# Reordering the loads and stores of a kernel's prologue, one encoder layer on one Trainium2 core

## The chip, the cores and the metric

The kernel runs on one core of one Trainium2 chip. The metric is the device time of one execution in microseconds (us). The time before the change is the median of 3 runs, 2337.61 us (2336.99 to 2337.95).

Names used below: PE is the matrix engine (TensorE), PEld its loading of stationary operands, DVE the vector engine, ACT the scalar engine, POOL GpSimd, SP the engine that here only issues transfers. A transfer (DMA) is issued by an engine's queue and carried by 16 DMA engines that all queues share.

## The reference, cut to what matters

One layer of an encoder over 4096 prompt frames and 32 sample frames, width 1024, all in float32:

```
h    = rmsnorm(x, norm_g)                      # x: 4096 x 1024 (and 32 x 1024)
proj = h @ w_in                                # w_in: 1024 x 5120 -> u | v | z_a | xb | z_b
v_n  = layernorm(v)
a    = u * (W_s v_n + b) * silu(z_a)           # W_s: 128 x 128 per head, masked in 64-blocks
b    = groupwise_linear(mean_window(xb) - xb) * scale * silu(z_b)    # w_pool: 4 groups of 256 x 256
x    = x + concat(a, b) @ w_out
y    = rmsnorm(x, final_g)
```

The windowed mean and the subtraction work along the frames and the group-wise linear map along the channels, so `w_pool` can be multiplied into the xb columns of `w_in` ahead of everything else. The product, a 1024 x 1024 matrix, is called `comb` in the kernel. For the sample frames the state of earlier frames (`state_pool`, 15 rows) goes through the same map.

## The kernel before, in words

**Products.** Each large product is split in 2 x 2 blocks and done with seven block products (numbered q = 0 to 6) in place of eight. Each float32 operand is split into a high part (a rounding copy on ACT, L120 for weights, L458 for tokens) and a low part (a subtraction on DVE, L82), and three of the four part products are made. One such block product of a stage is 12 matmuls of 128 x 512 (L194). The sums of blocks that the seven products need are subtractions and additions on DVE (L116 for weights, L486 to L495 for tokens).

**Stages.** First comes a prologue, then the v stage (tokens times the v columns of `w_in`, by pairs of 128-frame tiles), then the gate and pool stages over four blocks of 1024 frames, then the two output stages. The change touches the prologue alone, which ends about 56 us into the run.

**The prologue** (L519 to L548) does three things, interleaved over eight steps i = 0 to 7:

- *Rows of comb.* Row tile i of the xb columns of `w_in` (128 x 1024, loaded by `load_rows`, L254) is transposed by eight PE transposes (`comb_rows`, L407), copied out of PSUM (L411; DVE for i = 0 and 1, ACT from i = 2), and multiplied with `w_pool` in 16 matmuls (`comb_times`, L269). ACT copies the result into a tile `outs[i]` (L425), of the tag `xt` for i < 4 and `vt` from i = 4, and POOL's queue stores it to `comb` (L427). The loop traces the transposes of row i + 1 ahead of the matmuls of row i.
- *The v weights.* Four column chunks c = 0 to 3 of the v columns, two tiles of the tag `op` each (`load_v_weights`, L280 and L281), are made into the split operands of the seven products, which stay in `wv`. `PACE` says after which step how many of the 28 pieces are traced.
- *The first pair of token tiles.* `pairs[0].load` (L445) loads two tiles of x; `norms` squares and sums them on ACT (L302), makes the reciprocal root with short DVE instructions (L312, L87 to L92), and multiplies the tiles in place by it and by the gain `g_bc` (L315). Then PE transposes quarters of the tiles (L452) and `split` makes the operands, seven more `op` tiles.

Beside these, the state rows (`past`) and the last frames with the sample frames (`edge`) are loaded. The loop that follows (L550) multiplies pair n while it prepares pair n + 1.

**Buffers.** A tag has a fixed number of tiles, and a load into a tile waits until its last use is over: `vt` 4, `xt` 4, `op` 9, `h` 6.

**Order.** The source is not the order on the engines. A planner simulates the program and gives each engine the instruction that comes first in the source among those it takes to be ready, so later work can be drawn ahead of work that it believes is still waiting. `tc.keep_in_program_order` ties an instruction behind the one traced before it on its engine. Once planned, each engine works strictly in its given order. The dictionary `before` lists, for each step i, what is traced between the transposes of row i + 1 and the matmuls of row i: loads, norms, parts of `past`.

Of the kernel before, what the change touches and what calls it, by code (L numbers as in the profile page):

```python
# [8 lines left out]
F32 = mybir.dt.float32  # L9
# [3 lines left out]
AF = mybir.ActivationFunctionType  # L13
ALU = mybir.AluOpType

P = 128
# [20 lines left out]
def stream_step(ctx: ExitStack, tc, x_prompt, x_sample, state_pool, norm_g, w_in, ln_v_g, ln_v_b,  # L37
# [9 lines left out]
    nc = tc.nc  # L47
# [13 lines left out]
    comb = dram.tile([D, D], F32, name="comb")  # L61
# [16 lines left out]
    def small(tag, n, rows=P):  # L78
        return smallp.tile([P, 8], F32, tag=tag, name=tag)[:rows, :n]
# [4 lines left out]
    def rsqrt(a, n, rows=P):  # L84

        y, t = small("rs_y", n, rows), small("rs_t", n, rows)
        nc.vector.tensor_single_scalar(t.bitcast(I32), a.bitcast(I32), 1, ALU.logical_shift_right)  # L87
        nc.vector.tensor_scalar(y.bitcast(I32), t.bitcast(I32), -1.0, float(0x5F3759DF), ALU.mult, ALU.add)
        for _ in range(3):
            nc.vector.tensor_tensor(t, y, y, ALU.mult)  # L90
            nc.vector.scalar_tensor_tensor(t, t, -0.5, a, ALU.mult, ALU.mult)
            nc.vector.scalar_tensor_tensor(y, t, 1.5, y, ALU.add, ALU.mult)  # L92
        return y
# [16 lines left out]
    behind = []  # L110
# [108 lines left out]
    with ExitStack() as ph:  # L219
# [8 lines left out]
        def xtile(dt=F32):  # L228
            return xt_p.tile([P, D], dt, tag="xt", name="xt")

        def vtile():
            return v_p.tile([P, D], F32, tag="vt", name="vt")

        def op(dt=F32R):
            return op_p.tile([P, D], dt, tag="op", name="op")

        def half(dt=F32):
            return h_p.tile([P, HALF], dt, tag="h", name="h")

        def acc_tile():  # L240
            return ps_acc.tile([P, 512], F32, tag="acc", name="acc")
# [10 lines left out]
        def load_rows(i):  # L252
            rows_t[i] = vtile()
            nc.sync.dma_start(rows_t[i], w_in[0, i * P:(i + 1) * P, 3 * D:4 * D])  # L254
# [11 lines left out]
        def times(dst, g, rows):  # L266

            for ct in range(2):
                mm(dst, rows[ct], wraw[g // 2][:, 2 * (g % 2) + ct, :], start=ct == 0, stop=ct == 1)  # L269
# [6 lines left out]
        def load_v_weights(c):  # L276
            v_raws[c] = a, b = [t.rearrange("p (k e) -> p k e", e=P)
                                for t in (op(F32), op(F32))]
            c0 = D + c * P
            nc.sync.dma_start(a, w_in_v[:, :, c0:c0 + P])  # L280
            nc.sync.dma_start(b, w_in_v[:, :, c0 + 512:c0 + 512 + P])  # L281

        def make_v_weights():
            for c in range(4):
                a, b = v_raws.pop(c)
                cs = slice(c * P, (c + 1) * P)
                for step in weight_ops(a[:, :4], a[:, 4:], b[:, :4], b[:, 4:],
                                       lambda: half().rearrange("p (k e) -> p k e", e=P),
                                       lambda q: (wv[q][:, 0, :, cs], wv[q][:, 1, :, cs]), c < 2):
                    step()  # L290
                    yield

        def norms(xs_, vs_, behind=False):

            nx, nv, n = len(xs_), len(vs_), len(xs_) + len(vs_)
            rows = (xs_ + vs_)[0][1]
            a = small("na", n, rows)
            if xs_:
                ss = small("ss", nx, rows)
                for i, (xt, _) in enumerate(xs_):  # L300
                    junk = h_p.tile([P, D], BF16, tag="junk", name="junk", bufs=1)
                    nc.scalar.activation(junk[:rows], xt[:rows], AF.Square, accum_out=ss[:, i:i + 1])  # L302
            if vs_:
                st = smallp.tile([P, 2, 2, 6], F32, tag="bn", name="bn")
                mv = smallp.tile([P, 2, 2], F32, tag="mv", name="mv")
                for i, (v, _) in enumerate(vs_):
                    for z in range(2):
                        nc.vector.bn_stats(st[:rows, i, z, :], v[:rows, z * 512:(z + 1) * 512])
                    nc.vector.bn_aggr(mv[:rows, i, :], st[:rows, i].rearrange("p z c -> p (z c)"))
                nc.vector.tensor_scalar_add(a[:, nx:], mv[:rows, :nv, 1], EPS)  # L310
            if xs_:
                nc.vector.tensor_scalar(a[:, :nx], ss, 1.0 / D, EPS, ALU.mult, ALU.add)  # L312
            r = rsqrt(a, n, rows)
            for i, (xt, _) in enumerate(xs_):
                nc.vector.scalar_tensor_tensor(xt[:rows], xt[:rows], r[:, i:i + 1], g_bc[:rows], ALU.mult, ALU.mult)  # L315
            if vs_:
                nb = small("nb", nv, rows)
                nc.vector.scalar_tensor_tensor(nb, mv[:rows, :nv, 0], -1.0, r[:, nx:], ALU.mult, ALU.mult)
                for i, (v, _) in enumerate(vs_):
                    act = nc.scalar.activation(v[:rows], v[:rows], AF.Identity, scale=r[:, nx + i:nx + i + 1],  # L320
                                               bias=nb[:, i:i + 1])
                    if behind:
                        tc.keep_in_program_order(act)
# [34 lines left out]
        class Past:  # L358


            def load(self):
                self.st = half(), half()
                for z in range(2):
                    nc.gpsimd.memset(self.st[z][:HALO], 0.0)
                    nc.sync.dma_start(self.st[z][1:HALO], state_pool[0, 0, :, z * 512:(z + 1) * 512])
# [26 lines left out]
        pairs = []  # L392
        past = Past()
        PACE = (2, 4, 4, 4, 4, 4, 3, 3)

        def edge_load():
            nc.sync.dma_start(edge[:DEC], xs)
            nc.sync.dma_start(edge[DEC:m_edge], xp[SEQ - HALO:SEQ, :])
            nc.sync.dma_start(g_bc, norm_g[0].partition_broadcast(P))

        def comb_rows(i):
# [12 lines left out]
        outs = {}  # L414

        def comb_times(i, cols, halves=(0, 1)):
            if 0 in halves:
                outs[i] = xtile() if i < 4 else vtile()
            out = outs[i]
            for gp in halves:  # L420
                acc = acc_tile()
                for z in range(2):
                    s = [slice((2 * z + ct) * P, (2 * z + ct + 1) * P) for ct in range(2)]
                    times(acc[:, z * 256:(z + 1) * 256], 2 * gp + z, [cols[gp][:, x] for x in s])
                nc.scalar.copy(out[:, gp * 512:(gp + 1) * 512], acc)  # L425
            if 1 in halves:
                nc.gpsimd.dma_start(comb[i * P:(i + 1) * P, :], out)  # L427

        def columns():
            with nc.allow_non_contiguous_dma(reason="a few columns of constants"):  # L430
                tc.keep_in_program_order(nc.sync.dma_start(lvg, ln_v_g[0].rearrange("(h c) -> c h", c=P)))
                tc.keep_in_program_order(nc.sync.dma_start(lvb, ln_v_b[0].rearrange("(h c) -> c h", c=P)))
                tc.keep_in_program_order(nc.sync.dma_start(psc, pool_scale[0].rearrange("(h c) -> c h", c=P)))


        class Pair:
            def __init__(self, b, j):
                self.b, self.j, self.direct = b, j, b == 0 and j >= 2

            def load(self):  # L440
                self.x = []
                for z in range(2):
                    t0 = self.b * TB + z * HALF + self.j * P
                    xt = xtile()
                    nc.sync.dma_start(xt, xp[t0:t0 + P, :])  # L445
                    self.x.append(xt)

# [66 lines left out]
            def store(self, queue=nc.scalar):  # L514
                for z, v in enumerate(self.v):
# [2 lines left out]

        pairs += [Pair(b, j) for b in (1, 2, 3, 0) for j in range(4)]  # L519
        first_steps = pairs[0].operands()  # L520
        before = {0: [lambda: load_rows(3), lambda: load_v_weights(1)],
                  1: [lambda: load_rows(4)],
                  2: [lambda: load_rows(5), lambda: load_v_weights(2), past.load],
                  3: [lambda: load_rows(6), pairs[0].load],
                  4: [lambda: load_rows(7), edge_load],
                  5: [past.split, lambda: load_v_weights(3)],
                  6: [past.times, lambda: norms([(xt, P) for xt in pairs[0].x], []), pairs[1].load],
                  7: first_steps[:2]}
        weights = make_v_weights()
        load_rows(1)  # L530
        load_rows(2)
        load_v_weights(0)
        parts = comb_rows(0)
        for i in range(KT):
            if i == 0:
# [64 lines left out]
    def raw_tile(dt=F32):  # L600
        return raw_p.tile([P, D], dt, tag="raw", name="raw")
# [206 lines left out]
    with ExitStack() as ph:  # L808
# [231 lines left out]
        pairs = [[OutPair(z, i) for i in range(SEQ // (2 * P))] for z in range(2)]  # L1040
# [59 lines left out]
        for n in range(n_sets):  # L1100
# [9 lines left out]
            for m, (s, q) in enumerate(order):  # L1110
# [5 lines left out]
                if n == n_sets - 14 and m == 2:  # L1116
                    rows = raw_tile()[:DEC]
# [32 lines left out]
    with ExitStack() as ph:  # L1150
# [22 lines left out]
        outs = FewRows(lambda k: abT[k, :, SEQ:], lambda k: w_out_v[k], few_columns, KT - 1)  # L1173
# [92 lines left out]
```

## Time and profile before

| | |
|---|---|
| median of 3 runs | 2337.61 us |
| profiled execution, its own time | 2337.89 us |
| span of the profile | 2336.0 us |
| PE busy | 2317.2 us, 99% of the span |
| DVE, ACT, POOL busy | 1774.6, 889.3, 229.2 us |
| transfers | 457.42 MB, mean 196 GB/s |

The span runs from the first to the last instruction; the profiled execution's own time is 1.9 us longer. PE is busy in nearly all of the span, and a busy PE is not a PE at its peak. The average hides the prologue: in its first twentieth the 16 DMA engines move 316 and 310 GB/s, later mostly less than 200. "L254 SPq" is a transfer issued by SP from line 254; "xt<-acc" is written tile and read tile; "<-DMA vt<-in_w_in_dram" names what ended a wait. In the chain of waits, time is followed back from the last instruction to whatever released it.

### The profile page before, as it was taken

To read this page: it belongs to the slowest core of one execution; us is meant where nothing else is said; L and a number is where in the kernel's file an instruction comes from. 1 tells how busy PE (TensorE), PEld (TensorE's weight loads), DVE (VectorE), ACT (ScalarE), POOL (GpSimd) and SP (SyncE) were. 2 spreads that over 40 slices of the span, in tenths; PEclk is the share of its full clock that TensorE was granted. 3 is DMA by queue.
4 is the path that set the end of the run, shared out by engine and by line. 5 is a ranking of instruction groups with operands and counts; after the bars stand their busy time and mean duration, and the time that the engine had idled before them with its cause. 6 is when DMAs were issued, how large, how long until landed. Compare 5 with 4: busy or idle time off the path is not lost.

```text
span 2336.0 us, 32648 instructions
## 1 busy us (share of the span) xinstructions
PE 2317.2 (99%) x11936; PEld 1964.7 (84%) x11936; DVE 1774.6 (76%) x3285; ACT 889.3 (38%) x1596; POOL 229.2 (10%) x412
## 2 busy tenths in 40 slices
PE   8999999999999999999999999999999999999998
PEld 7888888888888888888877899999988777887887
DVE  6888777867887777868668877768776666588887
ACT  7544444334433333433334333334322222233343
POOL 1010000100112000111001211102110000000000
PEclk9999999999999999999999999999999999999999
DMA  8879977335447433483454474435584656846552
GB/s 316 310 269 280 281 244 251 111 108 189 145 170 271 147 127 130 129 328 120 164 164 149 165 276 146 143 94 173 192 323 163 211 201 198 342 163 202 178 167 91
DMA packets 329544, 457.42 MB, mean 196 GB/s; under 512 B 21964, under 2 KB 249932, under 8 KB 326696
## 3 DMA queue, kind: packets, MB, share of 16 engines
q1 hardware_dynamic: 277832, 366.91, 46.9%
q0 software_dynamic: 22288, 73.48, 8.4%
q10 hardware_dynamic: 29264, 14.94, 2.3%
q8 instruction: 94, 1.54, 0.3%
q14 instruction: 66, 0.54, 0.1%
HBM read 286.07 MB, written 169.21 MB: 195 GB/s over the span
## 4 chain that ended last, share of the span: by engine, by line
PE 94%; DMA 3%; DVE 2%; issue 1%; ACT 0%; SPq 0%; DVEq 0%; ACTq 0%
PE acc L194 64%; PE acc L691 8%; PE acc L692 8%; PE acc L693 8%; PE sp L939 2%; PE tr L452 1%; DMA wops<-wop 1%; DMA vt<-in_w_in_dram 1%; DVE wop L82 1%; DMA raw<-abT 1%; PE more L202 1%; DMA op<-in_w_in_dram 0%; PE acc L269 0%; PE acc L202 0%; DMA raw<-in_w_in_dram 0%
## 5 line engine op out<-in xcount | busy, mean ns | idle before, releaser
L194 PE MATMUL acc<-slot,wop 128*128 128x512 f32 (+1 forms) x6720 | 1260.1, 348 | 2.9 <-ACT t L173 1.0
L194 PEld LDWEIGHTS acc<-slot,wop 128*128 128x128 f32 x6720 | 1080.3, 188 | 163.2 <-DVE t L166 6.2
L82 DVE TENSOR_TENSOR wop<-raw,wop 128x512 fp32r<-128x512 f32 x520 | 355.8, 686 | 99.0 <-ACT wop L120 96.3
L120 ACT CAST wop<-raw 128x512 fp32r<-128x512 f32 x360 | 222.8, 622 | 349.2 <-PE acc L194 259.7
L691 PE MATMUL acc<-slot,wop 128*128 128x512 f32 x892 | 348.7, 391 | 1.8 <-DVE y L703 1.8
L693 PE MATMUL acc<-slot,wop 128*128 128x512 f32 x892 | 347.1, 389 | 0.0
L692 PE MATMUL acc<-slot,wop 128*128 128x512 f32 x892 | 347.0, 389 | 0.0
L194 PE MATMUL acc<-slot,op 128*128 128x512 f32 x1344 | 323.5, 395 | 0.1
L194 PEld LDWEIGHTS acc<-slot,op 128*128 128x128 f32 x1344 | 247.6, 188 | 51.8 <-DVE op L82 0.5
L703 DVE TENSOR_TENSOR y<-acc,y 128x512 f32<-128x512 f32 x235 | 159.1, 687 | 128.0 <-PE acc L693 126.9
L166 DVE TENSOR_TENSOR t<-acc,t 128x512 f32<-128x512 f32 (+1 forms) x320 | 185.7, 582 | 85.8 <-ACT t L175 44.9
L691 PEld LDWEIGHTS acc<-slot,wop 128*128 128x128 f32 x892 | 167.4, 188 | 47.0 <-ACT wop L656 11.9
L656 ACT CAST wop<-raw 128x512 fp32r<-128x512 f32 x160 | 99.6, 622 | 259.7 <-PE acc L693 251.9
L693 PEld LDWEIGHTS acc<-slot,wop 128*128 128x128 f32 x892 | 167.4, 188 | 35.2
L692 PEld LDWEIGHTS acc<-slot,wop 128*128 128x128 f32 x892 | 167.5, 188 | 34.2
L82 DVE TENSOR_TENSOR wop<-sum,wop 128x512 fp32r<-128x512 f32 x208 | 142.5, 686 | 57.6 <-ACT wop L120 57.0
L952 POOL DMA_DIRECT2D abT<-t x128 | 69.2, 541 | 822.3 <-DVE t L964 607.9
L120 ACT CAST wop<-sum 128x512 fp32r<-128x512 f32 x144 | 89.4, 622 | 152.6 <-PE acc L194 98.4
L975 DVE TENSOR_TENSOR t<-t 128x527 f32<-128x527 f32 (+3 forms) x160 | 111.0, 697 | 0.5
L656 ACT CAST wop<-sum 128x512 fp32r<-128x512 f32 x64 | 39.9, 623 | 131.6 <-PE acc L693 102.4
L116 DVE TENSOR_TENSOR sum<-raw 128x512 f32<-128x512 f32 x72 | 49.5, 687 | 36.8 <-DMA raw<-in_w_in_dram 34.9
L175 ACT COPY t<-acc 128x512 f32<-128x512 f32 (+1 forms) x80 | 40.1, 503 | 91.0 <-PE acc L194 90.5
(199 smaller groups left out, 1866.1 us busy)
## 6 DMA issues: line engine op xcount, KB each, us to landing
raw<-in_w_in_dram SPq DMA_DIRECT2D x110, 512.0 KB, 4.3
xops<-op SPq DMA_DIRECT2D x72, 512.0 KB, 5.7
abT<-t POOLq DMA_DIRECT2D x128, 256.0 KB, 3.7
raw<-abT SPq DMA_DIRECT2D x64, 512.0 KB, 4.7
slot<-xops SPq DMA_DIRECT2D x30, 1024.0 KB, 9.6
wops<-wop SPq DMA_DIRECT2D x56, 512.0 KB, 3.3
slot<-wops SPq DMA_DIRECT2D x14, 2048.0 KB, 9.9
xt<-in_x_prompt_dram SPq DMA_DIRECT2D x32, 512.0 KB, 4.4
```

What stands on the lines that cost most here:

```text
L82: return nc.vector.tensor_tensor(out, src, hi.bitcast(F32), ALU.subtract)
L116: less = lambda o, x, y: nc.vector.tensor_tensor(o, x, y, ALU.subtract)
L120: pair = nc.scalar.copy(hi, src), lo_part(lo, src, hi)
L166: add = lambda o, x, y: nc.vector.tensor_tensor(o, x, y, ALU.add)
L194: mm(acc, stationary(s, k), moving(m, k), start=fresh and n == 0, stop=n == len(terms) - 1, skip_group_check=True)
L656: nc.scalar.copy(t[:, 0], src)
L691: mm(acc, x[:, 0, k, :], w[:, k, 0, c], start=fresh and k == 0, stop=False, skip_group_check=True)
L692: mm(acc, x[:, 0, k, :], w[:, k, 1, c], start=False, stop=False, skip_group_check=True)
L693: mm(acc, x[:, 1, k, :], w[:, k, 0, c], start=False, stop=k == 3, skip_group_check=True)
L703: nc.vector.tensor_tensor(y, self.acc[bank], y, ALU.add)
L952: nc.gpsimd.dma_start(abT[row, :, t0:t0 + HALF], t[:, :HALF])
L975: tt(nxt[:, lo:HALO + m], s[:, lo:HALO + m], s[:, lo - step:HALO + m - step], ALU.add)
```

## The change

Seven edits, all in the prologue:

1. The stores of `outs[0]` to `outs[3]` leave POOL's queue at the end of each step. They are issued together by SP from step 5, in a new function `comb_store`. Rows 4 to 7 are stored as before.
2. Chunk 0 of the v weights is loaded ahead of row 2, and chunk 1 ahead of row 3.
3. The first token pair is loaded in step 1 in place of step 3, into two `op` tiles in place of `xt` tiles.
4. The gain `g_bc` gets a load of its own in step 2; it had been the last of the edge loads in step 4. The other edge loads move to step 6, behind the load of the second pair.
5. Chunk 3 is loaded in step 4, ahead of row 7, in place of step 5.
6. The norms of the first pair are traced in step 4 in place of step 6, and their two squares are tied behind the ACT instruction traced before them.
7. `past.load` stays in step 2, behind the loads of row 5 and of the gain.

```
@@ norms @@
-        def norms(xs_, vs_, behind=False):
+        def norms(xs_, vs_, behind=False, pinned=False):
...
-                    nc.scalar.activation(junk[:rows], xt[:rows], AF.Square, accum_out=ss[:, i:i + 1])
+                    square = nc.scalar.activation(junk[:rows], xt[:rows], AF.Square, accum_out=ss[:, i:i + 1])
+                    if pinned:
+                        tc.keep_in_program_order(square)
@@ edge_load @@
             nc.sync.dma_start(edge[DEC:m_edge], xp[SEQ - HALO:SEQ, :])
+
+        def g_load():
             nc.sync.dma_start(g_bc, norm_g[0].partition_broadcast(P))
@@ comb_times @@
-            if 1 in halves:
+            if 1 in halves and i >= 4:
                 nc.gpsimd.dma_start(comb[i * P:(i + 1) * P, :], out)
+
+        def comb_store():
+            for i in range(4):
+                nc.sync.dma_start(comb[i * P:(i + 1) * P, :], outs[i])
@@ Pair.load @@
-            def load(self):
+            def load(self, tile=xtile):
...
-                    xt = xtile()
+                    xt = tile()
@@ the prologue's loop @@
-        before = {0: [lambda: load_rows(3), lambda: load_v_weights(1)],
-                  1: [lambda: load_rows(4)],
-                  2: [lambda: load_rows(5), lambda: load_v_weights(2), past.load],
-                  3: [lambda: load_rows(6), pairs[0].load],
-                  4: [lambda: load_rows(7), edge_load],
-                  5: [past.split, lambda: load_v_weights(3)],
-                  6: [past.times, lambda: norms([(xt, P) for xt in pairs[0].x], []), pairs[1].load],
+        before = {0: [lambda: load_v_weights(1), lambda: load_rows(3)],
+                  1: [lambda: pairs[0].load(lambda: op(F32)), lambda: load_rows(4)],
+                  2: [lambda: load_v_weights(2), lambda: load_rows(5), g_load, past.load],
+                  3: [lambda: load_rows(6)],
+                  4: [lambda: load_v_weights(3), lambda: load_rows(7),
+                      lambda: norms([(xt, P) for xt in pairs[0].x], [], pinned=True)],
+                  5: [past.split, comb_store],
+                  6: [past.times, pairs[1].load, edge_load],
                   7: first_steps[:2]}
         weights = make_v_weights()
         load_rows(1)
+        load_v_weights(0)
         load_rows(2)
-        load_v_weights(0)
```

## The prediction

> **What bounds the kernel now.** I read the page, then the chain of waits over the first 70 us, then PE's order of time there, then tables by stretch of time. The page first:
>
> ```profile
> span 2336.0 us, 32648 instructions
> PE 2317.2 (99%) x11936; PEld 1964.7 (84%) x11936; DVE 1774.6 (76%) x3285; ACT 889.3 (38%) x1596; POOL 229.2 (10%) x412
> PE 94%; DMA 3%; DVE 2%; issue 1%; ACT 0%; SPq 0%; DVEq 0%; ACTq 0%
> ```
>
> PE bounds the run as a whole, so the prologue can give back only time in which PE waits or runs slowly. In the chain (start, duration, what) it is not PE that leads there:
>
> ```profile
> 3.19 5.89 DMA vt<-in_w_in_dram
> ...
> 10.28 1.73 PE acc L269 x8
> ...
> 12.18 9.59 DMA vt<-in_w_in_dram
> ...
> 30.79 7.44 DMA op<-in_w_in_dram
> ```
>
> Row 1 lands at 9.08 (3.19 + 5.89), row 4 at 21.77, and chunk 3 holds the chain to 38.23. PE in order of time (start, duration, then what):
>
> ```profile
> 11.85 1.04 PE L407 MATMUL tr<-ident,vt 128*128 128x128 f32 x8
> ...
> 16.18 1.04 PE L407 MATMUL tr<-ident,vt 128*128 128x128 f32 x8
> 17.05 3.62 PE L269 MATMUL acc<-op,h 128*128 128x256 f32 x16
> 21.90 1.06 PE L407 MATMUL tr<-ident,vt 128*128 128x128 f32 x8 [1.23 <-DMA vt<-in_w_in_dram]
> ...
> 31.56 0.66 PE L370 MATMUL tr<-ident,h 16*128 16x16 f32 x8
> 32.15 3.72 PE L269 MATMUL acc<-op,h 128*128 128x256 f32 x16
> 36.28 1.39 PE L407 MATMUL tr<-ident,vt 128*128 128x128 f32 x8 [0.41 <-ACT h L411]
> 37.59 1.06 PE L383 MATMUL acc<-op,h 128*16 128x256 f32 x16
> 38.58 3.72 PE L269 MATMUL acc<-op,h 128*128 128x256 f32 x16
> 44.15 0.66 PE L452 MATMUL tr<-ident,xt 128*128 128x128 f32 x4 [1.85 <-DVE xt L315]
> 44.64 0.60 PE L269 MATMUL acc<-op,h 128*128 128x256 f32 x2
> 45.44 0.80 PE L452 MATMUL tr<-ident,xt 128*128 128x128 f32 x4 [0.20 <-DVE xt L315]
> 46.03 4.74 PE L269 MATMUL acc<-op,h 128*128 128x256 f32 x14
> ...
> 52.84 10.79 PE L194 MATMUL acc<-slot,op 128*128 128x512 f32 x43
> 63.47 0.60 PE L452 MATMUL tr<-ident,xt 128*128 128x128 f32 x4
> ```
>
> Row 0's matmuls end at 12.01 (10.28 + 1.73), the last row's at 50.77 (46.03 + 4.74): 38.76 us. The work between, without waits, is six turns of a row at 0.87 (17.05 - 16.18), 5.22; seven times 16 matmuls at 3.62, 25.34; the state rows at 0.59 (32.15 - 31.56) and 0.99 (38.58 - 37.59), 1.58; two quarters of x at 0.49 (44.64 - 44.15), 0.98. That is 33.12, so 5.64 us are waiting or slowness: 1.23 for row 4, 0.41, 1.85 and 0.20 for the norm, and 1.57 because the last 14 matmuls took 4.74 where 14/16 of 3.62 is 3.17. The remaining 0.38 is spread. By stretch of time (columns: bounds, length, busy times of PE, PEld, DVE, ACT and POOL, granted clock, DMA share, GB/s):
>
> ```profile
> 4.00:16.00 12.00, 10.54 (x59) 8.73 (x58) 5.29 (x9) 3.18 (x6) 0.67 (x1) 1.00 1.07 366
> 16.00:38.30 22.30, 20.59 (x130) 17.15 (x128) 18.08 (x30) 19.52 (x39) 3.10 (x6) 1.00 1.07 390
> 18.45:21.86 3.41, 2.22 (x11) 1.61 (x9) 3.18 (x6) 3.41 (x8) 1.51 (x3) 1.00 1.06 378
> 42.34:45.76 3.42, 1.41 (x9) 1.04 (x10) 3.35 (x6) 3.35 (x8) 0.00 (x0) 1.00 0.24 96
> 45.76:49.17 3.41, 3.41 (x11) 2.78 (x10) 3.41 (x7) 3.41 (x8) 0.53 (x1) 0.50 0.42 157
> 12.05:50.81 38.76, 35.00 (x194) 28.68 (x192) 31.85 (x59) 33.71 (x68) 4.83 (x9) 0.96 0.91 336
> 56.04:2336.00 2279.96, 2267.86 (x11668) 1924.48 (x11668) 1736.19 (x3214) 850.39 (x1521) 223.18 (x396) 1.00 0.57 193
> ```
>
> The slowness is a half clock, 0.50, in the 3.41 us right after a stretch in which PE worked 1.41 of 3.42. To 38.3 us the DMA engines are full: a 512 KB load costs 0.524 MB / 366 = 1.43 us, from 16 us on 1.34.
>
> **The change part by part.** *The stores leave the load stream.* Four stores are 4 x 1.34 = 5.4 us of DMA time that no longer lies before chunk 3. *New order of loads.* Counted from row 1 at 9.08, the queue now holds chunk 0 (two loads), row 2, chunk 1, row 3, the first pair, row 4, chunk 2, row 5, the gain, row 6, chunk 3, row 7. Row 2 lands at 9.08 + 3 x 1.43 = 13.4, row 3 at 17.7, then with 1.34 row 4 at 21.7, row 5 at 25.7, row 6 at 28.4, chunk 3 at 31.1, row 7 at 32.5.
>
> PE reaches row 2 at 12.01, as its first transposes in the old trace show, and starts them at 13.5 now: a new wait of 1.5, and all that follows in PE's order waits with it. Then it needs row 3 at 13.5 + 0.87 + 3.62 = 18.0, row 4 at 22.5, row 5 at 27.0, row 6 at 31.5, row 7 near 36.6: each has landed 0.3 to 4 us before. So the old wait for row 4 goes, a larger one comes at row 2.
>
> *The first pair earlier, its squares tied.* It lands at 20.4 (17.7 + 2 x 1.34), the gain at 27.1. The squares come behind the copies of row 5, near 29. Rows of ACT and POOL before:
>
> ```profile
> 12.94 0.67 POOL L427 DMA_DIRECT2D comb<-xt  x1 [11.63 <-ACT xt L425]
> 16.07 0.62 ACT L120 CAST slot<-op 128x512 fp32r<-128x512 f32 x1 [1.42 <-DMA op<-in_w_in_dram]
> 32.56 1.06 ACT L302 ACTIVATE junk<-xt 128x1024 bf16<-128x1024 f32 x1 [2.12 <-DMA xt<-in_x_prompt_dram]
> 38.26 0.62 ACT L120 CAST slot<-op 128x512 fp32r<-128x512 f32 x1 [0.54 <-DMA op<-in_w_in_dram]
> 44.31 1.06 ACT L302 ACTIVATE junk<-xt 128x1024 bf16<-128x1024 f32 x1
> ```
>
> The square stood in ACT's order 2.12 us ahead of its data, and the casts behind it stood with it. There the second square came right behind the cast of 38.26 and PE could turn the pair at 44.15, 5.9 later. Now the second square stands near 30, so the pair is ready near 36, and PE asks for it near 42. So 1.85 and 0.20 go, and with them the empty stretch that I take for the cause of the half clock: 1.57 more. If this cover fails, up to 3.62 come back.
>
> [...]
>
> ```profile
> 19.86 1.28 DVE L82 TENSOR_TENSOR slot<-op,slot 128x512 fp32r<-128x512 f32 x2
> 29.11 0.69 DVE L116 TENSOR_TENSOR h<-op 128x512 f32<-128x512 f32 x1
> 113.56 0.70 PE L334 MATMUL tr<-ident,et 48*128 48x48 f32 x8
> ```
>
> *Buffers.* With the pair in `op` tiles, eight of nine are taken when chunk 2 is loaded; its second half waits for chunk 0's, whose last subtraction is the first of the two from 19.86, done about 20.5. It lands some 7 us later (the depth of the queue, from chunk 3: issued 30.79, landed 38.23), near 28; DVE first wants it at 29.11 in the old order. Hidden, 1 us of cover. *SP* issues four more transfers, ahead of them everything that PE needs; behind them stand the second pair and the edge frames. The `xt` tiles of the second pair come free only when the first two stores have landed. Stores end at 32.5 + 4 x 1.34 = 37.8, one store of POOL's between, the pair at 41.9. ACT squared it from 44.31 and PE turns it first at 63.47: hidden. POOL loses four issues of half a us; nothing waited for them. *Edge frames and gain:* PE turns the edge frames at 113.56; nothing.
>
> *ACT as the next limit.* From 12.05 to 50.81 it is busy 33.71, so it can't finish the same work before 45.8; of its 5.05 idle, 4.08 are the three waits above, which go. With 1.0 left it ends near 46.8. PE: 12.01 + 33.12 + 1.5 = 46.6. Two engines in fixed orders, this close, catch on each other; I charge 0.7, between 0 and 2.0 (the wait of 1.42 staying and another 0.6).
>
> *Behind the prologue.* From 50.77 to the products in series at 52.84 I change nothing. The rest holds 2279.96 - 2267.86 = 12.1 us of PE idle over 2280 us; a changed plan may shift a little of it, taken at 0, between -1 and +1.5 (an eighth).
>
> *Sum:* -5.64 + 1.5 + 0.7 = -3.4. The profiled execution took 2337.89, 1.9 more than its span, which the change leaves; 2334.5. The median of the runs is 0.28 lower, so 2334.2.
>
> **The rivals.**
>
> *Nothing is late (20%).* The planner may draw row 1's matmuls ahead of row 2's transposes. Then row 3 binds: 17.7 + 0.14 + 5 x 0.87 + 6 x 3.62 + 1.58 + 0.98 = 46.5; with nothing for ACT, and the 0.4 of idle that the stretch behind 50.77 holds beyond its work gone too, as well as the spread 0.38, it is -5.1: 2332.5. For it: all four early waits are on loads. Against: ACT's floor of 45.8 leaves it no slack.
>
> *The half clock stays or comes early (18%).* The new wait leaves PE some 2.0 us of work in a stretch of 3.4. The rows show 1.41 followed by half clock and 2.22 not; 2.0 is nearer the second. [...]
>
> *The stores don't go behind the loads (8%).* The planner orders by what it thinks ready. The stores are ready from 12 us on, while chunk 2's second half waits for a tile until 20.5. The price of a store beside loads is 1.34 by its bytes, or 2.8: chunk 1 had half landed at 16.07, two more loads should have brought row 4 at 18.9, and with the first store, from 12.94, between them it came at 21.77. Two stores at 2.8 put row 6 at 34.0, 2.5 after its need: 2336.7.
>
> *Slower: the second pair holds ACT (8%).* Its loads stand behind four stores on SP and on their landing. At 2.8 a store, with two of POOL's beside, the pair's first tile lands at 32.5 + 6 x 2.8 + 1.3 = 50.6. If its square keeps its place on ACT, ahead of the first pair's first cast, ACT stops. It decides from a landing at 44.31: from there the gain is gone, and at 50.6 it costs 6.3 (2343.9). The middle is 2340.7. Against: by bytes it lands ten us sooner, and the planner can see the wait.
>
> **How the numbers follow.** Forecast 46%, its own range 2332.8 to 2336.5 from the bounds of ACT, of the planned rest and of the load price (3 x 0.1). The range over the cases: 2331.8 to 2338.6; outside lie half of the slower case and the ends. A measurement here can tell about 0.2%, 4.7 us: faster is below 2332.9, which most of the first rival and the forecast's edge reach, 23%; slower is above 2342.3, part of the last, with something for a changed plan later in the run, 6%; within, 71%.
>
> **What would show it.** Right: row 2's transposes begin near 13.5 behind a load, no wait for row 4, the squares without a wait, the first turn of x right behind the matmuls before it, the clock at 1.00 throughout, the products in series near 49.4. Wrong: transposes that wait for rows 3 to 7, stores on SP ahead of chunk 3, a cast waiting behind the second pair's square, or waits behind 60 us that before does not have.

## The result and the profile after

| | before | changed |
|---|---|---|
| median of 15 runs each | 2336.99 us (2336.30 to 2338.51) | 2332.98 us (2330.78 to 2336.86) |
| profiled execution, its own time | 2337.89 us | 2333.04 us |
| span of the profile | 2336.0 us | 2331.2 us |

The ratio is 0.9983, with a 95% interval of 0.9976 to 0.9990: 4.0 us, or 0.17%, came off. That lies inside the 0.2% that the prediction called no change, and 1.2 us below its 2334.2. The changed file has a few lines more, so L407 of before is L411 here, L411 is L415, L425 is L429, L452 is L460 and L458 is L466.

The page of the changed kernel, its span and busy times:

```profile
span 2331.2 us, 32653 instructions
...
PE 2315.3 (99%) x11936; PEld 1964.9 (84%) x11936; DVE 1773.7 (76%) x3285; ACT 889.1 (38%) x1596; POOL 234.6 (10%) x408
```

The same 11,936 matmuls take PE 1.9 us less (2317.2 before); 1.57 of that is the half clock. The other 2.9 of the 4.8 us of span are waits. PE in order of time in the changed kernel (start, duration, what, and in brackets the idle time before it):

```profile
10.33 1.89 PE L269 MATMUL acc<-op,h 128*128 128x256 f32 x8
13.72 1.06 PE L411 MATMUL tr<-ident,vt 128*128 128x128 f32 x8 [1.49 <-DMA vt<-in_w_in_dram]
14.62 3.62 PE L269 MATMUL acc<-op,h 128*128 128x256 f32 x16
18.07 1.04 PE L411 MATMUL tr<-ident,vt 128*128 128x128 f32 x8
...
41.69 1.04 PE L460 MATMUL tr<-ident,op 128*128 128x128 f32 x8
42.56 3.62 PE L269 MATMUL acc<-op,h 128*128 128x256 f32 x16
...
48.25 2.33 PE L194 MATMUL acc<-slot,op 128*128 128x512 f32 x9
50.79 8.19 PE L194 MATMUL acc<-slot,op 128*128 128x512 f32 x33 [0.21 <-ACT op L466]
58.82 0.60 PE L460 MATMUL tr<-ident,xt 128*128 128x128 f32 x4
...
61.65 8.24 PE L194 MATMUL acc<-slot,op 128*128 128x512 f32 x35
```

There is one wait between the first row and the last: 1.49 us for row 2, at 13.72. None of the old waits is left, not even the small ones for the norm, and the last 16 matmuls take the full-clock 3.62. The last row ends at 46.18 (42.56 + 3.62), before at 50.77: 4.59 earlier.

Two later marks serve for all kernels below. The turn of the second pair (58.82 here, 63.47 before) is easy to find, but the planner puts it behind 45 of the first pair's matmuls in this kernel and behind 42 to 52 in others. The end of the first 84 of these matmuls (7 block products of 12) is nearly the same work everywhere (e10 has four more transposes ahead of it; in e4 no group ends there, and its mark is at 96): 61.65 + 8.24 = 69.89 here, and in the kernel before

```profile
66.30 8.01 PE L194 MATMUL acc<-slot,op 128*128 128x512 f32 x34
```

74.31. By this mark 4.42 us are gained. From it to the end of the span there are 2261.3 us after and 2261.7 before: in this pair of profiles the whole gain lies in the prologue.

By stretch of time (columns as in the prediction: bounds, length, PE, PEld, DVE, ACT, POOL, granted clock, DMA share, GB/s), first the kernel before:

```profile
12.00:42.00 30.00, 28.29 (x169) 23.72 (x166) 23.21 (x46) 25.81 (x51) 4.30 (x8) 1.00 1.05 383
```

and the changed one:

```profile
12.00:42.00 30.00, 28.51 (x173) 24.52 (x172) 26.61 (x52) 28.46 (x57) 2.24 (x4) 1.00 1.06 382
10.40:13.82 3.42, 1.93 (x10) 1.40 (x10) 1.41 (x3) 1.56 (x3) 0.00 (x0) 1.00 1.10 372
```

The DMA engines are as full as before and move the same bytes a second; what they move has another order. ACT does 28.46 of 30 us where it did 25.81: its waits for loads have turned into work. ACT in order of time, where the prediction looked:

```profile
29.41 1.10 ACT L302 ACTIVATE junk<-op 128x1024 bf16<-128x1024 f32 x1
...
30.93 1.11 ACT L302 ACTIVATE junk<-op 128x1024 bf16<-128x1024 f32 x1
...
41.68 1.06 ACT L302 ACTIVATE junk<-xt 128x1024 bf16<-128x1024 f32 x1
...
46.74 0.60 ACT L429 COPY vt<-acc 128x512 f32<-128x512 f32 x1
```

The first pair's squares run at 29.41 and 30.93 without a wait, and so does the second pair's at 41.68. The last row copy begins at 46.74. SP's queue, where a duration is the time that the issue took, waiting for room included:

```profile
20.73 0.38 SPq L281 DMA_DIRECT2D op<-in_w_in_dram  x1
...
29.40 3.43 SPq L435 DMA_DIRECT2D comb<-xt  x4
...
34.83 1.55 SPq L453 DMA_DIRECT2D xt<-in_x_prompt_dram  x2
```

The second half of chunk 2 waited for its tile until 20.73, and the four stores left from 29.40 on, behind every load that the rows and weights need.

### The profile page after: what moved, and what is told of

Read it like the earlier page. It is cut to its first block, busy times and chain, and to the rows that moved or that the text cites. A ratio compares the mean times of both kernels' runs of the same rounds, so it can differ in the third digit from the quotient of the medians.

```text
span 2331.2 us, 32653 instructions
## 1 busy us (share of the span) xinstructions
PE 2315.3 (99%) x11936; PEld 1964.9 (84%) x11936; DVE 1773.7 (76%) x3285; ACT 889.1 (38%) x1596; POOL 234.6 (10%) x408
## 4 chain that ended last, share of the span: by engine, by line
PE 93%; DMA 3%; DVE 2%; ACT 1%; issue 1%; SPq 0%; ACTq 0%; DVEq 0%
PE acc L194 62%; PE acc L700 9%; PE acc L702 9%; PE acc L701 9%; PE sp L948 2%; DMA wops<-wop 2%; PE tr L460 1%; PE acc L269 1%; DVE wop L82 1%; DMA raw<-in_w_in_dram 1%; PE more L202 1%; DMA vt<-in_w_in_dram 0%; DVE sum L116 0%; DMA raw<-abT 0%; PE tr L411 0%
## 5 line engine op out<-in xcount | busy, mean ns | idle before, releaser
L194 PE MATMUL acc<-slot,wop 128*128 128x512 f32 (+1 forms) x6720 | 1260.2, 348 | 3.9 <-ACT t L173 1.6
L194 PEld LDWEIGHTS acc<-slot,wop 128*128 128x128 f32 x6720 | 1080.4, 188 | 164.3 <-DVE t L166 6.8
L194 PE MATMUL acc<-slot,op 128*128 128x512 f32 x1344 | 323.3, 395 | 0.3 <-ACT op L466 0.2
L194 PEld LDWEIGHTS acc<-slot,op 128*128 128x128 f32 x1344 | 247.7, 188 | 51.9 <-ACT op L466 0.6
```

The lines of the kernel that those rows point to most:

```text
L194: mm(acc, stationary(s, k), moving(m, k), start=fresh and n == 0, stop=n == len(terms) - 1, skip_group_check=True)
```

## The experiments

All times are device us. "84" is the end of the first 84 matmuls of L194 in the kernel's profile and "rest" the span behind it. Kernels of one group ran on one chip beside the kernel before: group 1 (2336.89) e1 to e4, group 2 (2336.64) e5 to e9, group 3 (2336.67) e10 to e14.

| kernel | median (lowest to highest) | ratio to before, 95% | 84 | rest |
|---|---|---|---|---|
| before | 2336.99 (2336.30 to 2338.51) | | 74.31 | 2261.7 |
| changed | 2332.98 (2330.78 to 2336.86) | 0.9983 (0.9976 to 0.9990) | 69.89 | 2261.3 |
| e9, changed again | 2333.64 (2331.59 to 2334.37) | 0.9982 (0.9973 to 0.9991) | 69.68 | 2260.1 |
| e1, stores at once | 2336.56 (2334.85 to 2339.75) | 0.9999 (0.9990 to 1.0008) | 76.08 | 2261.8 |
| e5, stores late, by POOL | 2336.35 (2333.67 to 2339.17) | 0.9998 (0.9989 to 1.0007) | 71.94 | 2262.7 |
| e7, stores alone | 2331.66 (2330.47 to 2332.59) | 0.9978 (0.9969 to 0.9987) | 70.24 | 2259.7 |
| e14, stores alone again | 2332.04 (2330.72 to 2333.98) | 0.9983 (0.9974 to 0.9991) | 70.08 | 2260.0 |
| e2, squares not tied | 2334.17 (2332.62 to 2338.74) | 0.9992 (0.9983 to 1.0000) | 72.67 | 2259.3 |
| e4, gap filled | 2340.25 (2337.48 to 2341.25) | 1.0013 (1.0004 to 1.0022) | | |
| e3, rows ahead | 2332.27 (2330.65 to 2335.72) | 0.9981 (0.9972 to 0.9989) | 70.41 | 2260.7 |
| e6, rows ahead, ACT relieved | 2333.05 (2330.60 to 2334.22) | 0.9982 (0.9973 to 0.9991) | 70.52 | 2259.7 |
| e10, and second pair tied | 2332.99 (2331.44 to 2336.27) | 0.9987 (0.9978 to 0.9996) | 71.27 | 2259.6 |
| e11, stores and ties | 2332.64 (2330.93 to 2334.91) | 0.9985 (0.9976 to 0.9994) | 69.51 | 2262.9 |
| e12, and ACT relieved | 2333.92 (2331.80 to 2334.41) | 0.9988 (0.9979 to 0.9997) | 73.35 | 2258.9 |

The theory was that of the prediction: PE's waits in the prologue are for loads, the stores push the loads back, and an early norm removes the gap that costs the half clock. The rivals were that the stores' place doesn't matter, that the half clock stays or comes early, and that something other than PE's loads (ACT) sets the end.

### The stores where they were (e1)

The changed kernel, but POOL stores every row as soon as it is ready.

```
-            if 1 in halves and i >= 4:
+            if 1 in halves:
-                  5: [past.split, comb_store],
+                  5: [past.split],
```

> The changed kernel, but each of the first four rows of comb is stored by POOL as soon as it is made, as before the change; the other edits stay. If the stores' share of the DMA engines is what counted (four times 1.34 to 2.8 us of load time), rows 4 to 6 land late again, PE waits for them, and the first turn of the second pair, at 58.82 in the changed kernel, comes 1 to 3 us later, the time with it. If the early first pair did it all, it stays within 0.5 us of 58.82.

Measured: 2336.56, no different from before. All of the gain is gone. Its POOL queue, then its PE in order of time, then its table by stretch of time:

```profile
14.36 0.67 POOL L431 DMA_DIRECT2D comb<-xt  x1 [13.05 <-ACT xt L429]
```

```profile
22.42 1.29 PE L411 MATMUL tr<-ident,vt 128*128 128x128 f32 x8 [3.00 <-DMA vt<-in_w_in_dram]
23.51 5.11 PE L269 MATMUL acc<-op,h 128*128 128x256 f32 x16
```

```profile
19.71:23.12 3.41, 0.70 (x7) 0.73 (x8) 2.34 (x4) 1.40 (x4) 1.50 (x3) 1.00 1.02 414
23.12:26.53 3.41, 3.41 (x12) 2.79 (x11) 0.00 (x0) 1.14 (x2) 0.00 (x0) 0.50 1.05 365
```

With the first store issued at 14.36, PE waits 3.00 us for row 3, and behind the wait the clock is halved for 3.41 us: 5.11 for the 16 matmuls that take 3.62. In the trace's records of transfers row 3 lands at 22.29, 4.54 us behind the load before it (17.75); in the changed kernel it is 1.30 (17.86 and 16.56). So in this execution the first store of 512 KB cost row 3 some 3.2 us. The profiled execution was this kernel's slowest, 3.2 us above its median, and its row 1 already landed at 10.51 where the changed kernel's transposes began at 9.43; so 76.08, which is 6.2 behind the changed kernel where 1 to 3 were expected, overstates a usual execution, and the 3.2 may too (e5 has a smaller price).

### Stores late, but by POOL (e5)

```
-                nc.sync.dma_start(comb[i * P:(i + 1) * P, :], outs[i])
+                nc.gpsimd.dma_start(comb[i * P:(i + 1) * P, :], outs[i])
```

> The changed kernel with the four late stores issued by POOL in place of SP. If it is only the time of the stores that counts, the turn of the second pair stays within 1 us of 58.82 and the time within 1 us of the changed kernel's. If being in SP's order matters (the stores then can't run beside loads), row 7 or chunk 3 land later, PE or ACT waits for them, and 1 to 3 us are lost.

Measured: 2336.35, again no gain that can be told from the kernel before, where the changed kernel beside it made 2333.64. The POOL queue of this kernel, then its PE:

```profile
12.41 0.67 POOL L435 DMA_DIRECT2D comb<-xt  x1 [11.11 <-ACT xt L429]
18.68 0.53 POOL L435 DMA_DIRECT2D comb<-xt  x1 [5.60 <-DVE slot L82]
```

```profile
18.29 1.06 PE L411 MATMUL tr<-ident,vt 128*128 128x128 f32 x8 [0.54 <-DMA vt<-in_w_in_dram]
...
32.85 1.06 PE L411 MATMUL tr<-ident,vt 128*128 128x128 f32 x8 [1.38 <-DMA vt<-in_w_in_dram]
```

Traced in step 5, the stores still leave at 12.41 and 18.68 (the other two at 24.04 and 29.02), because the planner draws them ahead as soon as their data is there and POOL has nothing else to do. On SP they left from 29.40. So the planner's order does not put the stores behind the loads; SP's occupied queue does. The prediction's rival of 8% had this mechanism right, for another queue.

Two things here are weaker than in e1. The first store costs less: row 3 lands 2.06 behind the load before it (18.15 and 16.09), 0.8 more than in the changed kernel, and the next three loads are 1.2 to 1.3 late, near the 1.34 that the store's bytes take. And only a part of what e5 loses lies in the prologue. The rows end at 48.58, 2.40 behind the changed kernel's, and the first 84 matmuls at 71.94, which is still 2.4 ahead of the profile of the kernel before; its rest is 1.0 longer than there and 2.5 longer than e9's. Why the rest is longer was not traced.

### The stores alone (e7, e14)

The kernel before with its old order of loads, its norms in step 6 and no ties; only the stores go late by SP, and the first pair goes to `op` tiles because the `xt` tiles are held by stores that have not yet left.

```
-            if 1 in halves:
+            if 1 in halves and i >= 4:
+        def comb_store():
+            for i in range(4):
+                nc.sync.dma_start(comb[i * P:(i + 1) * P, :], outs[i])
-                  3: [lambda: load_rows(6), pairs[0].load],
+                  3: [lambda: load_rows(6), lambda: pairs[0].load(lambda: op(F32))],
-                  5: [past.split, lambda: load_v_weights(3)],
+                  5: [past.split, lambda: load_v_weights(3), comb_store],
```

> The kernel before with one part of the change: the four stores late by SP, behind chunk 3, and for that the first pair in operand tiles; the loads keep their old order, the norm its old place, the squares untied. If the stores' share of the DMA time was nearly all of the loss, the load of row 4 and of the pair come 1.3 to 2.8 us sooner each and the turn of the second pair comes 3 to 4.6 us before the old 63.47. If the early pair and the tie are needed as well, ACT's wait for the pair and the gap on PE ahead of its first turn stay, and it gains 0 to 2 us.

> e7_stores_alone unaltered, beside the three above on one chip. If its lead over the changed kernel (2331.66 against 2333.64 on one chip) is its own and not of one group of runs, it stays 4.5 to 5.5 us below the kernel before; if it was chance, 3 to 4 us.

Measured: 2331.66 and 2332.04, 5.0 and 4.6 below the kernel before. This is at least the whole gain of the change; e14 lies within the 4.5 to 5.5 expected of a lead that is the kernel's own. The other tile of the first pair belongs to this edit and was not tried apart; e1 and e5 have it too and show no gain. PE in order of time in e7:

```profile
26.32 0.66 PE L407 MATMUL tr<-ident,vt 128*128 128x128 f32 x4 [0.45 <-ACT h L411]
...
41.59 0.66 PE L456 MATMUL tr<-ident,op 128*128 128x128 f32 x4 [0.53 <-DVE op L315]
...
43.34 3.19 PE L269 MATMUL acc<-op,h 128*128 128x256 f32 x14
...
62.70 7.54 PE L194 MATMUL acc<-slot,op 128*128 128x512 f32 x32
```

No row is waited for behind row 1, since the old order has row 2 in the second place and no store lies between the loads. The wait for the norm shrinks from 1.85 to 0.53 by itself, and the last 14 matmuls run at full clock, 3.19 for 4.74. The rows end at 46.53, 0.35 behind the changed kernel's, and the first 84 matmuls at 70.24, also 0.35 behind.

### The changed kernel again (e9)

> The changed kernel unaltered, beside the others on one chip, to compare with. The turn of the second pair within 1.2 us of 58.82 (loads of one size landed up to 1.2 us apart between profiles), the time 4 us below the kernel before.

Unaltered, beside e5 to e7: 2333.64, 3.0 below the kernel before where 4 was expected, and 1.70 us of wait for row 2. Against e7 in the same group it is 2.0 us slower. Its ratio interval overlaps with e7's, and its profiled execution was its fastest, so profiles of the two can't be set against each other to a microsecond. The stores alone are not slower than the change in any pair of groups, but by how much they are faster is not settled: 0.6 to 2.0 us.

### Squares not tied (e2)

```
-                      lambda: norms([(xt, P) for xt in pairs[0].x], [], pinned=True)],
+                      lambda: norms([(xt, P) for xt in pairs[0].x], [])],
```

> The changed kernel without the tie of the two squares. The planner then draws the first square ahead of casts, near 17 us, where its data has not landed (19.1 us). If ACT has no slack, as its continuous work from 16.55 us on in the changed kernel says, ACT's wait of about 2 us goes through to the turn of the second pair: 1 to 2 us later than 58.82. If the tie is idle, less than 0.4 us.

Measured: 2334.17. Two rows of what its ACT waited for (total us, times, longest), and PE in order of time:

```profile
ACT junk L302 <- DMA op<-in_x_prompt_dram: 2.0, 1, 2.0
...
ACT junk L302 <- DMA xt<-in_x_prompt_dram: 1.3, 1, 1.3
```

```profile
50.38 0.65 PE L460 MATMUL tr<-ident,op 128*128 128x128 f32 x4 [0.72 <-ACT ppast L392]
...
64.44 8.23 PE L194 MATMUL acc<-slot,op 128*128 128x512 f32 x35
```

Without the tie ACT stands 2.0 us for the first pair, as it stood 2.12 before, and 1.3 for the second; PE gets it in pieces of up to 0.72, and the first 84 matmuls end at 72.67, 2.78 behind the changed kernel's. In the medians of different groups the difference is 1.2, and the intervals overlap. So in the trace the tie does what the prediction said, though e7 shows that with the old order it isn't needed.

### The gap filled (e4)

The kernel before, with 14 transposes of the identity, whose result nothing reads, tied into PE's order where the gap was.

```
+        def fill():
+            t = tr_tile()
+            for _ in range(14):
+                tc.keep_in_program_order(nc.tensor.transpose(t[:, :P], ident, ident))
-                  7: first_steps[:2]}
+                  7: [fill] + first_steps[:2]}
```

> The kernel before, with 14 transposes of the identity, some 1.5 us, put on PE into its gap ahead of the first turn of the first pair (42.3 to 44.15 us); their output is not used. If that gap brings on the half clock, the clock stays 1.00, the last 14 matmuls take 3.2 in place of 4.74 and the time falls by about 1.6. [...]

PE in order of time, and the stretches around and behind the gap:

```profile
42.92 1.69 PE L525 MATMUL tr<-ident 128*128 128x128 f32 x14
...
46.97 3.62 PE L269 MATMUL acc<-op,h 128*128 128x256 f32 x16
```

```profile
43.88:47.30 3.42, 2.15 (x17) 1.70 (x16) 3.42 (x4) 3.37 (x8) 0.00 (x0) 1.00 0.17 69
...
45.91:49.32 3.41, 2.84 (x16) 2.58 (x16) 3.41 (x7) 3.41 (x8) 0.53 (x1) 1.00 0.28 111
```

The half clock is gone: the last matmuls take 3.62 for 16, at a clock of 1.00. The first stretch has the 3.42 us of the one ahead of the half clock in the kernel before, and the place of the gap lies in it. Of its 2.15 us of work 0.73 are the fill, which ends at 44.61; without them 1.42 are left, as the 1.41 in the kernel before. So the gap was the cause, as far as one profile of each kernel can show it. But the kernel is 3.4 us slower than before, where a gain was expected. Its first 96 matmuls of L194 end at 78.06, those of before at 77.52, though its row 0 had ended 1.07 later (13.08, not 12.01); so within the prologue the fill gave about half a us. Behind that, PE waits at places where it didn't before, such as 0.78 at 811.2 and 0.37 at 820.0. Adding instructions changed the plan of what follows; what exactly in the plan costs the rest stays open.

### Rows ahead of the weights (e3)

Row 2 ahead of chunk 0, row 3 ahead of chunk 1, row 4 ahead of the first pair, to take away the new wait.

```
-        before = {0: [lambda: load_v_weights(1), lambda: load_rows(3)],
-                  1: [lambda: pairs[0].load(lambda: op(F32)), lambda: load_rows(4)],
+        before = {0: [lambda: load_rows(3), lambda: load_v_weights(1)],
+                  1: [lambda: load_rows(4), lambda: pairs[0].load(lambda: op(F32))],
...
-        load_v_weights(0)
         load_rows(2)
+        load_v_weights(0)
```

> The changed kernel with row 2 loaded ahead of chunk 0, row 3 ahead of chunk 1 and row 4 ahead of the first pair; every engine but SP keeps its order. PE's new wait of 1.49 us for row 2 goes. If only PE's waits count, the turn of the second pair comes 1.5 us sooner, near 57.3, and the time falls by 1.5. If ACT is the next limit (about 1.1 us of idle left behind 12.26 us in the changed kernel), at most 1.1 is gained, and nearer 0.5, with PE waiting for ACT in the last rows.

Measured: 2332.27, not distinguishable from the changed kernel. PE in order of time, and its stretch from 46 to 52:

```profile
26.36 1.06 PE L411 MATMUL tr<-ident,vt 128*128 128x128 f32 x8 [0.75 <-DMA vt<-in_w_in_dram]
...
42.22 3.62 PE L269 MATMUL acc<-op,h 128*128 128x256 f32 x16
...
51.32 8.19 PE L194 MATMUL acc<-slot,op 128*128 128x512 f32 x33 [0.48 <-ACT op L466]
```

```profile
46.00:52.00 6.00, 5.14 (x30) 3.52 (x28) 5.59 (x13) 5.97 (x13) 0.53 (x1) 1.00 0.90 324
```

The wait for row 2 is gone; half of it comes back at row 5, and the rows end only 0.34 earlier (45.84). Then PE waits for ACT, which is busy 5.97 of 6.00 us, and the first 84 matmuls end 0.52 later than in the changed kernel. Behind the rows ACT has no slack in this kernel, and what PE gained ahead of it was lost there.

### ACT relieved, and ties (e6, e10, e11, e12)

e6 is e3 with the copies of the state rows on DVE instead of ACT. e10 (the second fence) adds a tie for the second pair's squares.

```
-                    nc.scalar.copy(self.st[g // 2][:HALO, c:c + 256], acc[32 * g:32 * g + HALO, :256])
+                    nc.vector.tensor_copy(self.st[g // 2][:HALO, c:c + 256], acc[32 * g:32 * g + HALO, :256])
```

```
-        norms([(xt, P) for xt in pairs[1].x], [])
+        norms([(xt, P) for xt in pairs[1].x], [], pinned=True)
```

> The order of loads of e3_rows_ahead, and the four copies of the state rows out of PSUM (1.53 us of ACT near 39 us) made by DVE in place of ACT. If ACT was what kept e3_rows_ahead from a gain, its last copies come 1 to 1.5 us sooner and the turn of the second pair falls from 59.35 to 57.5 to 58.5, so below the changed kernel's 58.82. If the loads limit, it stays at 59.3.

> e6_rows_ahead_act_relieved with the squares of the second pair tied in ACT's order too, behind the first pair's last parts. In e6 ACT waited 2.1 us for the second pair's data in front of the first pair's casts, and PE then 1.7 us for ACT. If that wait is all that took e6's gain back, the turn of the second pair falls from 60.03 to 57.8 to 58.8; if DVE or the loads hold it, it stays above 59.5.

What e6's ACT waited for, and its stretch from 46 to 54:

```profile
ACT junk L302 <- DMA xt<-in_x_prompt_dram: 2.1, 2, 1.9
```

```profile
46.00:54.00 8.00, 6.27 (x30) 4.30 (x29) 8.00 (x15) 8.00 (x17) 0.53 (x1) 1.00 0.80 308
```

The rows end at 45.04, 1.14 earlier than in the changed kernel, and the first 84 matmuls at 70.52, 0.63 later. In e6 ACT waits 2.1 us for the second pair (the mechanism that the prediction gave for its slower case, at a third of its size), and then ACT and DVE are both busy for all 8 us, while PE works 6.27. So with ACT relieved DVE has no slack either. With the tie of e10 that wait is gone, and PE waits for operands instead:

```profile
51.56 8.84 PE L194 MATMUL acc<-slot,op 128*128 128x512 f32 x36 [1.38 <-ACT op L466]
```

The second pair's turn came at 60.03 in e6 and 60.34 in e10, later than a gain would have put it.

e11 is e7 with the first pair's norms in step 5 and both pairs' squares tied; e12 adds the copies on DVE.

```
-                  5: [past.split, lambda: load_v_weights(3), comb_store],
-                  6: [past.times, lambda: norms([(xt, P) for xt in pairs[0].x], []), pairs[1].load],
+                  5: [past.split, lambda: load_v_weights(3), comb_store,
+                      lambda: norms([(xt, P) for xt in pairs[0].x], [], pinned=True)],
+                  6: [past.times, pairs[1].load],
...
-        norms([(xt, P) for xt in pairs[1].x], [])
+        norms([(xt, P) for xt in pairs[1].x], [], pinned=True)
```

> e7_stores_alone (stores late, old order of loads) with the first pair's norm traced in step 5 and the squares of both pairs tied. The norm's remaining wait on PE (0.53 and 0.20 us) should go and ACT keep its order: the turn of the second pair from 59.84 to 58.5 to 59.3. If the tie is no use where the data lands in time, it stays within 0.4 of 59.84.

> e11_stores_and_ties with the four copies of the state rows on DVE. If ACT is the limit of that version, 0.5 to 1.5 us sooner than e11; if DVE is by then, no gain or a loss up to 1 us.

Neither beats e7 or e14. The second pair's turn came at 60.08 in e11 (behind 52 matmuls there), where ties of no use would have left it, and at 63.84 in e12, later than either case expected. e11 has the earliest end of the first 84 matmuls of all (69.51) and then a half clock far behind the prologue; e12 has one in the first products. Stretches of e11, then of e12:

```profile
1476.29:1479.70 3.41, 1.67 (x14) 1.45 (x13) 0.98 (x2) 1.64 (x4) 0.00 (x0) 1.00 0.43 142
1479.70:1483.11 3.41, 3.41 (x18) 3.41 (x17) 3.38 (x6) 1.48 (x4) 0.00 (x0) 0.50 0.02 5
```

```profile
50.34:53.75 3.41, 1.44 (x7) 0.78 (x6) 3.24 (x6) 2.61 (x5) 0.00 (x0) 1.00 0.59 239
53.75:57.16 3.41, 3.41 (x10) 2.62 (x9) 3.41 (x6) 3.37 (x7) 0.00 (x0) 0.50 0.79 324
```

## Why the prediction was right, and where it was off

**The new wait for row 2.** Predicted 1.5, measured 1.49. The working by place in the queue (9.08 + 3 x 1.43 = 13.4) holds: the transposes began at 13.72, with 13.5 predicted, and all later rows were there in time. The planner did not draw the matmuls of row 1 ahead, so the rival "nothing is late" fell, although its time, 2332.5, lies nearer to the measured 2332.98 than the forecast does.

**The old waits and the half clock.** 1.23, 0.41, 1.85, 0.20 and 1.57 are all gone. That the gap caused the half clock was argued from one row; e4 supports it, since the clock stays at 1.00 when the gap is filled and the stretch with the gap would hold 1.42 us of work without the fill, as the 1.41 of before.

**The new wait and the clock.** The prediction held the stretch with the new wait, estimated at 2.0 us of work, to be nearer 2.22 than 1.41. It held 1.93 and was not followed by a half clock, so the rival in which the half clock stays or comes early fell.

**The squares, the stores, the second pair.** Predicted near 29, measured 29.41, without a wait; the tile for chunk 2 free about 20.5, measured 20.73; the second pair's square without a wait, measured so at 41.68, so the slower rival fell here. The price of a store beside loads, 1.34 or 2.8, did not enter this kernel because the stores are behind. The runs leave it open: row 3 came 3.2 late in e1, the loads behind the first store 1.2 in e5. The 2.8 itself rests on one landing: against e7, which has the same loads without the early stores, the first store of the kernel before made row 4 come 2.84 later but row 5 only 1.51.

**The step that was mis-sized** is the work term, 33.12, and with it the charge of 0.7 for ACT. From row 0's end (12.22 = 10.33 + 1.89) to the last row's end (46.18) there are 33.96 us after; without the 1.49 of waiting, 32.47. The prediction added seven durations of 3.62, but the next transposes start 3.45 after a row's matmuls do (18.07 - 14.62): in the rows of the profile the end of a matmul overlaps with what follows, unless that waits. From start to start the seven rows' matmuls take 24.54 in place of 25.34, while the turns take 5.48 in place of 5.22. So the work was 0.54 too large and the excess in the kernel before that much too small; another 0.11 went because x is now turned in one piece. ACT's 0.7 was not charged: its last row copy began at 46.74, as late as the prediction had it, but PE waited for ACT nowhere in the rows, and 0.21 behind them. Work, x and ACT make 1.35 us together, about the 1.2 by which the forecast lay above the median; that the two agree so well is partly luck, since the medians of the changed kernel in its two groups differ by 0.7.

**Where it had the right sum for a mixed reason.** The prediction spread the gain over the order of loads, the early norm with its tie, and the stores. In the medians all of it is with the stores: while POOL issues them no gain can be seen (e1, e5), and with them late on SP, and little else, all of it is there (e7, e14). The profiles are less clear-cut, since e5 keeps about half of the gain in the prologue. The new order of loads brings the wait for row 2 and gives nothing that can be measured. The early norm removes 0.73 us of wait in the trace; e11, which adds it to e7, ends its first 84 matmuls 0.6 to 0.7 earlier than e14 and e7, but no median shows a gain. The prediction had seen that ACT is the next limit (floor 45.8), and e3 fits that; in e6 and e10, with ACT relieved, DVE is as full. In all three the rows end 0.3 to 1.1 us earlier than in the changed kernel, and the first 84 matmuls end no earlier.

**The rest of the run.** It was taken at 0, between -1 and +1.5. In the change it is -0.4 by the two profiles. But over the kernels tried, "rest" runs from 2258.9 to 2262.9, and two profiles of the changed kernel alone differ by 1.2. The bounds were too narrow for an edit that changes the plan: e4 lost 1.8 there by its mark at 96 matmuls, and e7 gained 2.0. One place of it can be seen, changed kernel first, then e7:

```profile
1479.21 1.72 PE L194 MATMUL acc<-slot,wop 128*128 128x264 f32 x12 [1.57 <-ACT t L173]
```

```profile
1478.02 1.73 PE L194 MATMUL acc<-slot,wop 128*128 128x264 f32 x12 [0.30 <-ACT t L173]
```

1.27 us at one instruction 1.4 ms behind the edit. Why the wait there differs was not traced, and it may be what makes e7 the faster of the two in its group.

## What to carry to other kernels

Where a queue of loads is full and PE runs on what it brings, look first at what else shares the engines: a store placed among the loads delayed them by 1.2 us (e5) to 3.2 us (e1), and moving four stores behind the loads gave the whole gain in the medians (5.0 us in e7, 4.6 in e14), while the order among the loads was worth nothing that could be measured, with ACT and DVE right behind PE (ACT busy 5.97 of 6.00 us in e3, DVE all 8.00 in e6). Which queue issues a transfer decides its time as much as its place in the source, if a planner orders by readiness: traced in step 5, the first store left at 12.41 by POOL (e5) and at 29.40 by SP (the changed kernel). And to size the work between two marks, add start-to-start distances, not durations: 3.45 us here where the duration of a row's matmuls is 3.62.

## What the runs showed of the hardware that was not expected

**The half clock came behind stretches in which PE still worked.** Four profiles show a granted clock of 0.50 for 3.41 us within the run. In the 3.41 or 3.42 us before, PE worked 0.70 (e1), 1.41 (before), 1.44 (e12) or 1.67 us (e11). Three stretches of this length had no half clock behind them: with 1.93 us of work in the changed kernel, with 1.72 in e9 (from 11.14), and with 1.67 in this one of e5, behind which the 16 matmuls from 14.13 take the full-clock 3.62:

```profile
10.32:13.73 3.41, 1.67 (x11) 1.22 (x10) 1.40 (x3) 1.62 (x3) 0.67 (x1) 1.00 1.09 360
```

In these stretches PE had waited 3.00 us (e1), 1.85 (before) and 1.97 (e12) where the half clock followed, and 1.49 (changed), 1.70 (e9) and 1.75 (e5) where it did not. It cost 1.57 us in the kernel before. Why the 1.67 of e11 was followed by it and that of e5 not was not tested, and one profile of a kernel does not show how often it pays for a given wait.

**A store among loads can cost more than its bytes, but need not.** In e1 from 13 to 24 us, in 40 equal slices, the transfers ran at

```profile
GB/s 354 341 356 357 339 331 331 333 348 346 298 102 104 158 199 244 343 343 358 343 343 417 387 432 387 417 432 432 402 402 447 417 417 387 462 395 341 291 344 302
```

For about 1.4 us (five slices of 0.275, from 16.0 on) the sum falls to 102 to 244 GB/s from some 340, around the first packet of the first store at 16.8. Against 340 that is 0.25 MB not moved (5 x 340 - 807 GB/s, times 0.275 us), or 0.7 us of the 1.9 that row 3 came later beyond the store's own 1.34. Why the sum falls, and where the other 1.2 us lie, was not tested. It is not the rule: the same view around the first store of the kernel before (12 to 25 us) has no slice below 312 GB/s and that of e5 (11 to 22 us) none below 313, and in e5 the store's price was about its bytes. Single landings also scatter by about 1 us without any store: in e7 one load came 2.44 behind the one before it (21.78 and 19.34). So the sizes given here for one store are those of single executions.
